# Moving the memory values ahead of the attention, reordering a router, moving a branch, and keeping the experts' sum with features on partitions

## The chip, the cores and the metric

The kernel runs on one core of a Trainium2 chip. The metric is the time of one execution on the device, in microseconds; the time before and after is the median of several executions. A profile comes from one execution of its own. All times below are microseconds unless marked ns.

## What is computed

Two transformer blocks, one after the other, on one sequence of 256 tokens with 1024 features, in fp32. Cut to what the change touches:

```python
# first block
x = x + g1 * mixed                                  # attention (MLA and neighbourhood) @ w_out
t = modulate(rmsnorm(x, norm_ffn_g), sh2, sc2)      # rows t of 1024 features
g_sel = argmax(t @ w_rg + b_rg)                     # router: one of 4 groups
e_logits = (t @ w_re + b_re)[group g_sel]           # top 2 of the group's 4 experts
y = sum over the 2 chosen experts of weight * ((silu(t @ wg[e]) * (t @ wu[e])) @ wd[e])
x = rmsnorm(x + g2 * y, final_norm_g)
# second block
h = rms_norm(x, g_mix)
proj = h @ w_in        # convolution, stick-breaking attention, queries xq, gates
k, v = split(rms_norm(mem, g_mem) @ w_mem_kv)       # memory keys and values, 256 x 1024 each
...                    # cross attention of xq on k, v; gated sum; w_out; MLP
```

The memory keys and values depend on no result of the first block. There are 16 experts with 512 hidden features.

## The kernel before

The order of the work is written by hand: each engine runs its instructions in the order of the code, and waits where an operand isn't there. Weights come from HBM once, as pieces of about 1 MB, in the order of the list `plan`; `pump()` issues the next loads while slots of the SBUF pool are free (`take` and `give` take and return a slot of 4 KB per partition, 24 in all). SP issues them.

Most products run through a stream `S` of jobs. A piece is split into a rounded high part (line 207 on ACT, or 205 on DVE) and the rest (line 208 on DVE), and three matmuls make one product: `step` (line 233) holds the activations and moves 512 weight columns, `step_w` (line 272) holds the weights and moves 256 tokens. `S.fine` (line 252) is the same as `step`, as a generator that emits a few matmuls at a time. PSUM has eight banks: four "b" banks for short-lived results and four "acc" banks for accumulation; a new tile of a kind waits until the oldest user of its bank is done.

The stages, in order: adaLN and memory keys, with the first half of the memory values; `w_in` products of the first block (the last job is nv); attention by heads, with `latents()` as side work; `w_out` (J_wo[0], J_wo[1]); router; 16 experts in pairs; the second block.

- The second half of the memory values is the job J_mv[1]. It is loaded after w_out and emitted in portions between the steps of the router by `fill(n)` (lines 1075, 1084, 1128, 1192), and goes to HBM by line 1193.
- `router_const()` (line 856) multiplies the shift sh2 with the router's weights (16 matmuls of 20 columns) and adds the result to `br` (line 861). It is called last in `latents()`.
- Router: `xa_T(c)` transposes x (features to partitions) and scales it; `logits` (line 1049) accumulates 20 columns; line 1107 scales them to `lg`; lines 1117 to 1126 rank groups and experts on DVE; lines 1131 to 1133 count with matmuls into the bank `bl`; line 1136 makes the place of each token in its expert's list, and `slots_of(n)` (line 1143) the one-hot map `D[n]` of four experts; `tot` (line 1148) reads `bl` last. An expert has 64 places.
- `xn` is x divided by its root mean square, `xh` and `xlo` its high part and rest (GpSimd, line 1104); their columns are reordered. `gather(n)` (line 1181) multiplies them with `D[n]` into `xg[n]`, tokens of four experts, features on partitions; two "b" banks at a time.
- `bcast_rows(i, t)` (line 981) spreads a row of the modulation over all partitions by matmuls of one row; the one of g2 into `gm` is in expert 1.
- Experts: `moe_up` (line 1269), gate (lines 1283, 1284), `moe_hT`, `moe_down` (line 1303), `moe_out` (lines 1317 to 1320: weighted outputs RA, split to RB), `moe_comb(p)` (line 1328) adds a pair's outputs to the sum with the map `DT`. The sum `yb[tt][dh]` has tokens on partitions and fills the four "acc" banks. `add_x` (line 1063) adds the residual x to it by a matmul with the identity.
- `beyond()` (line 1402) is a branch on a flag that says whether an expert has more tokens than places; its body isn't entered for these inputs. It stands after expert 14 (`e == NE - 2`). All engines pass line 1404 together.
- Tail: the sum is copied to x (lines 1540, 1541), `fgm` is the product of two norm gains (line 1543), GpSimd multiplies x by `fgb` (line 1548), x is transposed (line 531), `hilo` (lines 546 on ACT, 547 on DVE) makes its halves `uh`, `ul`, and `S.step()` begins the `w_in` products of the second block, into "acc" banks. Then the sums of squares, the root and its broadcast `rb`.

Of the kernel before, what the change touches and what calls it, by code (L numbers as in the profile page):

```python
# [9 lines left out]
F32 = mybir.dt.float32  # L10
# [79 lines left out]
def body(tc, d, out, dbg=None, stop=None):  # L90
# [87 lines left out]
    class Stream:  # L178
# [63 lines left out]
        def fine(self, job):  # L242

            while self.pos < job.end:
                job, key, a, k, kg, first, last, done = self.g[self.pos]
                s = self.prepared.pop(self.pos)
                if first:
                    job.accs = job.acc()
                for m, (hi, lo) in enumerate(job.lhs):
                    for kk in range(kg):  # L250
                        for j, (x, w) in enumerate(((hi, 0), (lo, 0), (hi, 1))):
                            T.matmul(job.accs[m], x(k + kk), s[:, w, kk, :], start=first and kk == 0 and j == 0,  # L252
                                     stop=last and kk == kg - 1 and j == 2)
                    if last:
                        job.evac(m, job.accs[m])
                    if m == len(job.lhs) - 1:
                        give(s)
                        self.pos += 1
                    yield

# [157 lines left out]
    plan_mod(1, range(4, 8))  # L418
    P_uq = [plan_w(("uq", c), d["w_uq"], 384, 384 * c, 384) for c in range(2)]
# [6 lines left out]
    P_memv.append(plan_w(("mv", 1), d["w_mem_kv_2"], 1024, 1536, 512))  # L426
# [166 lines left out]
    J_mv = [Job(P_memv[c], 512, mlhs, ev_memv(c), acc=(lambda: [bank(), bank()]) if c else None) for c in range(2)]  # L593
# [161 lines left out]
    for j in (J_kvl, J_ql, J_nq, J_nk, J_nv):  # L755
        S.add(j)
# [84 lines left out]
    give(*hT["x"], *hT["c"])  # L841
    dump("nqT", nqT)
# [24 lines left out]
    def latents():  # L867
# [37 lines left out]
        router_const()  # L905
# [95 lines left out]
    for j in J_wo + J_mv[1:]:  # L1001
        S.add(j)
# [32 lines left out]
    def xa_T(c):  # L1035
        for k0, bk in transposed_pairs(lambda tt, k: x[:, tt, 512 * c + k:512 * c + 512:4], 4):
# [72 lines left out]
    keep(1)  # L1109
# [18 lines left out]
    fill(1)  # L1128
# [17 lines left out]
    slots_of(0)  # L1146
    tot = smal([128, 16], "tot")
# [755 lines left out]
```

## Time and profile before

| what | value |
|---|---|
| median of three runs | 1071.27 (1068.00 to 1072.09) |
| the profiled execution's own time | 1069.21 |
| span of the profile | 1067.4 |
| granted TensorE clock over the span | 0.992 |
| PE busy | 1037.5 (97%) |
| DVE, ACT, POOL busy | 593.8 (56%), 437.4 (41%), 92.4 (9%) |
| HBM read | 249.73 MB |

The span runs from the first to the last instruction of the profiled execution; the 1.8 us around it are in that execution's own time. Matmuls of one group overlap their neighbours by a little in the rows, since their ends are modelled: the pace of a stretch is read from the starts of its groups. L12 is line 12 of the kernel before.

### The profile page before, as it was taken

How to read it: one execution, taken by the hardware profiler on the slowest of the kernel's cores; microseconds unless marked ns; L12 is line 12 of the kernel's file. 1: busy time of each engine (PE TensorE's matmuls, PEld its weight loads, DVE VectorE, ACT ScalarE, POOL GpSimd, SP SyncE). 2: the span in 40 equal slices, each digit the busy share in tenths (PEclk: the TensorE clock that was granted, in tenths of full speed). 3: DMA queues.
4: the chain of work that ended last, by engine and by line, in shares of the span. 5: the costliest groups of instructions: out<-in, count | busy, mean ns of one | idle time of the engine just before them, and what ended most of it. 6: DMA issues, size and time to landing. Idle time of an engine off the chain costs nothing.

```text
span 1067.4 us, 14961 instructions
## 1 busy us (share of the span) xinstructions
PE 1037.5 (97%) x6035; PEld 777.6 (73%) x6035; DVE 593.8 (56%) x928; ACT 437.4 (41%) x744; POOL 92.4 (9%) x100
## 2 busy tenths in 40 slices
PE   6999999999999999998999999999999999999998
PEld 5587866657744343433699789998888889999996
DVE  5565237775624342523666556766456677666544
ACT  5664115674423131312534684444443144443332
POOL 0000303000201010100104452000000000000000
PEclk9999999999999999999999999999999999999999
DMA  9999741625789999999924324537566555455511
GB/s 333 402 354 346 222 150 54 251 105 240 273 344 419 418 419 420 419 419 412 383 70 160 129 78 151 175 119 260 174 204 229 197 197 197 160 196 201 193 41 40
DMA packets 82410, 254.95 MB, mean 239 GB/s; under 512 B 4760, under 2 KB 8344, under 8 KB 67616
## 3 DMA queue, kind: packets, MB, share of 16 engines
q1 hardware_dynamic: 80848, 249.22, 62.7%
q0 software_dynamic: 1488, 4.72, 1.4%
q8 instruction: 49, 0.80, 0.3%
q14 instruction: 25, 0.20, 0.1%
HBM read 249.73 MB, written 4.19 MB: 238 GB/s over the span
## 4 chain that ended last, share of the span: by engine, by line
PE 73%; DMA 19%; DVE 4%; ACT 2%; SPq 1%; issue 1%; DVEq 0%; ACTq 0%
PE acc L233 35%; PE acc L272 14%; DMA raw<-in_w_up 9%; PE b L272 8%; DMA raw<-in_w_down 6%; PE b L1269 3%; PE b L531 2%; DMA raw<-in_w_mod 2%; PE b L640 2%; DMA raw<-in_w_in 1%; PE acc L964 1%; PE b L252 1%; SPq L141 1%; DVE split L208 1%; DVE sm L940 1%; PE b L1610 1%
## 5 line engine op out<-in xcount | busy, mean ns | idle before, releaser
L208 DVE TENSOR_TENSOR split<-raw,split 128x1024 fp32r<-128x1024 f32 (+2 forms) x226 | 267.8, 1212 | 92.7 <-ACT split L207 90.5
L207 ACT ACTIVATE split<-raw 128x1024 fp32r<-128x1024 f32 (+2 forms) x170 | 168.7, 1034 | 63.0 <-DMA raw<-in_w_uq 15.7
L272 PE MATMUL acc<-uh,split 128*128 128x256 f32 x640 | 123.2, 288 | 1.4 <-ACT uh L546 1.4
L1269 PE MATMUL b<-raw,xg 128*64 128x512 f32 x512 | 116.1, 602 | 3.8 <-DVEq L1404 3.8
L272 PEld LDWEIGHTS acc<-uh,split 128*128 128x128 f32 x640 | 102.5, 193 | 2.7 <-ACT uh L546 1.8
L233 PE MATMUL acc<-split,uh 128*128 128x512 f32 x320 | 101.3, 392 | 0.0
L272 PE MATMUL b<-fh,split 128*128 128x256 f32 x512 | 93.8, 283 | 0.3 <-DVE split L208 0.3
L272 PE MATMUL acc<-ul,split 128*128 128x256 f32 x320 | 91.3, 285 | 0.1
L233 PE MATMUL acc<-split,hidT 128*128 128x512 f32 x384 | 88.4, 389 | 0.0
L1269 PEld LDWEIGHTS b<-raw,xg 128*64 128x64 f32 x512 | 35.8, 138 | 71.7 <-issue 69.9
L233 PEld LDWEIGHTS acc<-split,hidT 128*128 128x128 f32 x384 | 71.6, 188 | 14.6
L272 PEld LDWEIGHTS b<-fh,split 128*128 128x128 f32 x512 | 80.4, 192 | 0.8 <-DVE split L208 0.5
L272 PE MATMUL b<-fl,split 128*128 128x256 f32 x256 | 72.4, 283 | 0.0
L233 PEld LDWEIGHTS acc<-split,uh 128*128 128x128 f32 x320 | 60.1, 188 | 12.8
L272 PEld LDWEIGHTS acc<-ul,split 128*128 128x128 f32 x320 | 61.9, 193 | 0.7 <-DVE ul L547 0.6
L233 PE MATMUL acc<-split,ul 128*128 128x512 f32 x160 | 62.3, 390 | 0.0
L1303 PE MATMUL b<-raw,RA 128*64 128x512 f32 x256 | 58.5, 596 | 1.2 <-DMA raw<-in_w_down 1.2
L1317 DVE SCALAR_TENSOR_TENSOR RA<-b,wc,gm 64x512 f32<-64x512 f32 x32 | 24.0, 750 | 60.4 <-PE b L1303 59.9
L1318 ACT ACTIVATE RB<-RA 64x512 fp32r<-64x512 f32 x32 | 20.1, 628 | 77.6 <-DVE RA L1317 77.5
L272 PEld LDWEIGHTS b<-fl,split 128*128 128x128 f32 x256 | 49.1, 192 | 0.3
L1830 ACT ACTIVATE hid<-b 128x512 f32<-128x512 f32 x16 | 9.5, 595 | 91.3 <-PE b L272 91.3
L1303 PEld LDWEIGHTS b<-raw,RA 128*64 128x64 f32 x256 | 17.8, 137 | 37.6 <-issue 32.2
(414 smaller groups left out, 1738.7 us busy)
## 6 DMA issues: line engine op xcount, KB each, us to landing
raw<-in_w_up SPq DMA_DIRECT2D x48, 1024.0 KB, 13.2
raw<-in_w_down SPq DMA_DIRECT2D x48, 1024.0 KB, 16.2
raw<-in_w_in SPq DMA_DIRECT2D x46, 1024.0 KB, 7.5
raw<-in_w_gate SPq DMA_DIRECT2D x32, 1024.0 KB, 19.8
raw<-in_w_mod SPq DMA_DIRECT2D x24, 1024.0 KB, 8.2
raw<-in_w_out SPq DMA_DIRECT2D x8, 1024.0 KB, 6.1
raw<-in_w_mem_kv SPq DMA_DIRECT2D x7, 1024.0 KB, 11.1
raw<-in_w_conv_out SPq DMA_DIRECT2D x4, 1024.0 KB, 5.1
```

The costliest lines, as they stand in the source:

```text
L141: nc.sync.dma_start(t, src)
L207: A.activation(s[:, 0], src, AF.Copy)
L208: V.tensor_tensor(s[:, 1], src, s[:, 0].bitcast(F32), op=OP.subtract)
L233: T.matmul(job.accs[m], x(k + kk), s[:, w, kk, :], start=job.start and first and kk == 0 and j == 0, stop=job.stop and last and kk == kg - ...
L252: T.matmul(job.accs[m], x(k + kk), s[:, w, kk, :], start=first and kk == 0 and j == 0, stop=last and kk == kg - 1 and j == 2)
L272: T.matmul(bk[:, o:o + 256], s[:, w, kk, 128 * b:128 * b + 128], x(k + kk), start=first and b % per == 0 and r == 0 and kk == 0 and j == 0 ...
L531: T.transpose(bk[0:m, i * 128:i * 128 + p], s, ident)
L640: T.matmul(modacc[Tn][32 * g:32 * g + 32, :], cond[:, k, :], w[:, g // 2, 512 * (g % 2):512 * (g % 2) + 512] if Tn == 2 else w[:, g, :], s ...
L1269: T.matmul(b[64 * j:64 * j + 64, :], lt, raw((nm, e, k // 4))[:, k % 4, :], start=(k == 0), stop=(k == 7), skip_group_check=True)
L1303: T.matmul(b[64 * j:64 * j + 64, :], t[:, k, :], raw(("d", e, k // 2))[:, k % 2, 512 * dh:512 * dh + 512], start=(k == 0), stop=(k == 3), ...
L1317: V.scalar_tensor_tensor(RA[r, dh, :], b[r, :], wc[r, dh, e % 2:e % 2 + 1], gm[r, dh], op0=OP.mult, op1=OP.mult)
L1318: A.activation(RB[r, 0, dh, :], RA[r, dh, :], AF.Copy)
```

## The change

The job J_mv[1] moves into the stream behind nv, ahead of the attention, and its loads move with it; `fill` and `fine` go. `router_const()` moves to the start of the router, `add_x(0)` to `add_x(3)` and the broadcast of g2 into it. `xn` goes: `x_hi` (ACT) and `x_lo` (DVE) make the halves from x, without reordering; the gather takes every fourth column instead. The first gather uses four "b" banks at once and takes the parts that need the last rest at the end. The experts' sum becomes `yT`, features on partitions: `moe_comb` holds 128 columns of RB and moves 256 columns of DT. The first `sq` job of the second block accumulates in "b" banks. The branch and its hint move from expert 14 to expert 13. In the tail, `hilo` reads the sum directly, and `y_back` transposes it to tokens on partitions afterwards, for the sum of squares and the product with `fgb`. The branch's body (not entered) is adapted to the new layout and left out here.

```diff
...
+    P_memv.append(plan_w(("mv", 1), d["w_mem_kv_2"], 1024, 1536, 512))
     P_uq = [plan_w(("uq", c), d["w_uq"], 384, 384 * c, 384) for c in range(2)]
...
-    P_memv.append(plan_w(("mv", 1), d["w_mem_kv_2"], 1024, 1536, 512))
...
-    for j in (J_kvl, J_ql, J_nq, J_nk, J_nv):
+    for j in (J_kvl, J_ql, J_nq, J_nk, J_nv, J_mv[1]):
...
+    mvt[1] = take([128, 2, 512], F32, "mvt")
+    S.run(J_mv[1])
+    G.dma_start(mvd[:, :, 512:1024], mvt[1])
+    give(memTh, memTl, mvt[1])
...
         give(st["kvl"], st["kvT"])
-        router_const()
...
     def xa_T(c):
-        for k0, bk in transposed_pairs(lambda tt, k: x[:, tt, 512 * c + k:512 * c + 512:4], 4):
+        bks = [bank() for _ in range(2)]
+        for tt in range(2):
+            for k in range(4):
+                o = 256 * (k % 2) + 128 * tt
+                T.transpose(bks[k // 2][:, o:o + 128], x[:, tt, 512 * c + k:512 * c + 512:4], ident)
...
-    yb = [[None, None], [None, None]]
-    xres = x
-    def add_x(tt, dh):
-        T.matmul(yb[tt][dh], ident, xres[:, tt, 512 * dh:512 * dh + 512], start=False, stop=False, skip_group_check=True)
+    yT = [None] * 4
+    def y_of(k):
+        return yT[k // 2][:, 256 * (k % 2):256 * (k % 2) + 256]
+    def add_x(k, first=False):
+        if first and k % 2 == 0:
+            yT[k // 2] = bank("acc")
+        for tt in range(2):
+            T.matmul(y_of(k)[:, tt * 128:(tt + 1) * 128], x[:, tt, k * 128:(k + 1) * 128], ident,
+                     start=first and k % 2 == 0 and tt == 0, stop=False, skip_group_check=True)
     la[0] = 4
     S.run(J_wo[1])
     la[0] = 2
-    mvt[1] = take([128, 2, 512], F32, "mvt")
-    mvg = S.fine(J_mv[1])
-    def fill(n):
-        for _ in range(n):
-            next(mvg, None)
-    fill(3)
+    router_const()
...
-    fill(2)
-    logits(1, 0)
-    logits(1, 1)
+    add_x(0, True)
+    add_x(1, True)
+    logits(1, 0, 1)
     give(xaT)
     keep(4)
-    xn = take([128, 2, 1024], F32, "xn2")
+    gm = take([128, 4, 512], F32, "gm")
     xh = take([128, 2, 1024], F32R, "xh")
     xlo = take([128, 2, 1024], F32R, "xlo")
     keep(1)
-    def fo(t):
-        return t.rearrange("p (h j q) -> p h j q", h=2, j=4)
-    def fi(t):
-        return t.rearrange("p (h q j) -> p h j q", h=2, j=4)
-    V.tensor_scalar(fo(xn[:, 0, :]), fi(x[:, 0, :]), r2[:, 0:1], None, op0=OP.mult)
-    for tt in range(2):
-        A.activation(fo(xh[:, tt]), fi(x[:, tt, :]), AF.Identity, scale=r2[:, tt:tt + 1])
-    A.activation(fo(xn[:, 1, :]), fi(x[:, 1, :]), AF.Identity, scale=r2[:, 1:2])
-    for tt in range(2):
-        G.tensor_tensor(xlo[:, tt], xn[:, tt], xh[:, tt].bitcast(F32), op=OP.subtract)
+    def x_hi(hi):
+        for tt in range(2):
+            A.activation(hi[:, tt], x[:, tt, :], AF.Identity, scale=r2[:, tt:tt + 1])
+    def x_lo(hi, lo):
+        for tt in range(2):
+            V.scalar_tensor_tensor(lo[:, tt], x[:, tt, :], r2[:, tt:tt + 1], hi[:, tt].bitcast(F32), op0=OP.mult, op1=OP.subtract)
+    x_hi(xh)
     lg = smal([128, 2, 20], "lg")
     for tt in range(2):
         V.scalar_tensor_tensor(lg[:, tt], lgb[:, 20 * tt:20 * tt + 20], r2[:, tt:tt + 1], br, op0=OP.mult, op1=OP.add)
     dump("lg", lg)
-    keep(1)
+    add_x(2, True)
+    add_x(3, True)
+    bcast_rows(1, gm)
...
-    fill(1)
     bl = bank()
...
     slots_of(0)
+    x_lo(xh, xlo)
     tot = smal([128, 16], "tot")
     V.tensor_reduce(tot, bl[:, 32:64].rearrange("p (t e) -> p e t", t=2), AX.X, OP.add)
...
     def halves(n):
         hi, lo = take([128, 2, 1024], F32R, "xh"), take([128, 2, 1024], F32R, "xlo")
-        for tt in range(2):
-            A.activation(hi[:, tt], xn[:, tt], AF.Copy)
-            G.tensor_tensor(lo[:, tt], xn[:, tt], hi[:, tt].bitcast(F32), op=OP.subtract)
+        x_hi(hi)
+        x_lo(hi, lo)
...
+        def part(q, bks, i):
+            h, tt = (xh, xh, xlo, xlo)[i], i % 2
+            for k in range(4):
+                T.matmul(bks[k // 2][:, 256 * (k % 2):256 * (k % 2) + 256],
+                         h[:, tt, 512 * q + k:512 * q + 512:4], Dn[tt],
+                         start=(i == 0 and k % 2 == 0), stop=(i == 3), skip_group_check=True)
...
+        if n == 0:
+            bq = [[bank(), bank()] for _ in range(2)]
+            for i in range(3):
+                for q in range(2):
+                    part(q, bq[q], i)
+            for q in range(2):
+                part(q, bq[q], 3)
+                evac(q, bq[q])
+            return
+        for q in range(2):
+            bks = [bank(), bank()]
+            for i in range(4):
+                part(q, bks, i)
+            evac(q, bks)
             yield
-    fill(8)
-    G.dma_start(mvd[:, :, 512:1024], mvt[1])
-    give(memTh, memTl, mvt[1])
...
     def moe_comb(p):
         for dh in range(2):
-            for tt in range(2):
-                if p == 0:
-                    yb[tt][dh] = bank("acc")
-                for w in range(2):
-                    T.matmul(yb[tt][dh], DT[:, (2 * dh + tt) * 128:(2 * dh + tt + 1) * 128], RB[:, w, dh, :],
-                             start=(p == 0 and w == 0), stop=(p == 7 and w == 1), skip_group_check=True)
+            for w in range(2):
+                for i in range(4):
+                    k = 4 * dh + i
+                    if p == 0 and w == 0 and k in (4, 6):
+                        yT[k // 2] = bank("acc")
+                    T.matmul(y_of(k), RB[:, w, dh, 128 * i:128 * i + 128], DT[:, 256 * dh:256 * dh + 256],
+                             start=(p == 0 and w == 0 and k in (4, 6)), stop=(p == 7 and w == 1), skip_group_check=True)
...
+            J2[nm, c] = Job(P_in2[nm, c], 512, evac=ev_sqk(nm == "sk", c), rhs=urhs,
+                            acc=(lambda: [bank(), bank()]) if (nm, c) == ("sq", 0) else None)
...
+        if e == NE - 3:
+            tc.mark_branch_hint_location("over", "LikelyTaken", engines=[mybir.EngineType.PE])
...
-                gm = take([128, 4, 512], F32, "gm")
-                bcast_rows(1, gm)
...
-        if e == NE - 2:
+        if e == NE - 3:
             beyond()
...
-    add_x(0, 0)
+    add_x(4)
+    add_x(5)
     moe_down(NE - 2)
-    add_x(1, 0)
     moe_down(NE - 1)
-    add_x(0, 1)
-    add_x(1, 1)
+    add_x(6)
+    add_x(7)
     raw_done("x")
     S.hold = None
     S.ahead(1)
+    fgm = smal([128, 8], "fgm")
+    V.tensor_tensor(fgm, col("final_norm_g"), col("g_mix_2"), op=OP.mult)
     moe_comb(NE // 2 - 1)
     give(gm, RA, RB)
-    x = take([128, 2, 1024], F32, "x1")
     lim[:] = [4, 2]
     ss3 = smal([128, 4], "ss3")
-    for tt in range(2):
-        A.activation(x[:, 0, 512 * tt:512 * tt + 512], yb[0][tt], AF.Copy)
-        V.tensor_copy(x[:, 1, 512 * tt:512 * tt + 512], yb[1][tt])
...
-    xf = take([128, 2, 1024], F32, "x1f")
-    for tt in range(2):
-        G.tensor_tensor(xf[:, tt], x[:, tt], fgb, op=OP.mult)
     uh = s2["uh"] = take([128, 8, 256], F32R, "uh")
     ul = s2["ul"] = take([128, 8, 256], F32R, "ul")
-    for k0, bk in transposed_pairs(lambda tt, k: x[:, tt, k * 128:(k + 1) * 128], 8):
-        for kk in range(2):
-            hilo(uh[:, k0 + kk], ul[:, k0 + kk], bk[:, kk], fgm[:, k0 + kk:k0 + kk + 1])
-        if k0:
-            S.step()
-        if 0 < k0 < 6:
-            tt = k0 // 2 - 1
-            sumsq(ss3[:, tt:tt + 1], x[:, tt, :])
-    give(x)
-    x = xf
+    yt = take([128, 8, 256], F32, "yt")
+    x = take([128, 2, 1024], F32, "x1f")
+    def y_halves(dh):
+        for k in range(4 * dh, 4 * dh + 4):
+            hilo(uh[:, k], ul[:, k], y_of(k), fgm[:, k:k + 1])
+            if k in (1, 3):
+                S.step()
+        A.activation(yt[:, 4 * dh:4 * dh + 2].rearrange("p a t -> p (a t)"), yT[2 * dh], AF.Copy)
+        V.tensor_copy(yt[:, 4 * dh + 2:4 * dh + 4].rearrange("p a t -> p (a t)"), yT[2 * dh + 1])
+    def y_back(dh):
+        s = slice(512 * dh, 512 * dh + 512)
+        for tt in range(2):
+            bk = trans_bank([yt[:, 4 * dh + i, tt * 128:(tt + 1) * 128] for i in range(4)])
+            sumsq(ssh[:, dh, tt:tt + 1], bk)
+            V.tensor_tensor(x[:, tt, s], bk, fgb[:, s], op=OP.mult)
+    y_halves(0)
+    y_halves(1)
+    y_back(0)
+    S.step()
+    y_back(1)
+    give(yt)
+    V.tensor_tensor(ss3[:, 0:2], ssh[:, 0], ssh[:, 1], op=OP.add)
...
```

## Rows read from the trace of the kernel before

**Rows 1.** Windows: length; busy PE, PEld, DVE, ACT, POOL; granted clock; DMA share; GB/s.
```profile
280.00:300.00 20.00, 17.36 (x90) 14.41 (x91) 10.44 (x34) 11.97 (x16) 5.46 (x3) 0.83 0.67 231
...
480.00:500.00 20.00, 15.78 (x68) 4.81 (x64) 6.97 (x11) 4.91 (x7) 0.00 (x0) 0.91 1.01 416
```

**Rows 2.** Chain of waits that ended last, two of its links (columns: start; us; link).
```profile
107.02 5.94 PE acc L272 x48
...
134.78 5.68 PE acc L233 x24
```

**Rows 3.** Timeline in the attention (columns: start; us; engine; line; operation; idle before).
```profile
205.74 1.86 PE L859 MATMUL acc<-wr,sh 128*128 128x20 f32 x16
...
207.96 0.17 DVE L861 TENSOR_TENSOR br<-br,acc 128x20 f32<-128x20 f32 x1
...
208.69 0.43 DVE L938 TENSOR_TENSOR b<-b,raw 128x256 f32<-128x256 f32 x1 [0.57 <-PE b L926]
...
210.78 1.13 PE L929 MATMUL b<-kT,qT 96*128 96x512 f32 x2 [1.09 <-DVE b L938]
```

**Rows 4.** Timeline of the router, w_out's end to the first expert.
```profile
274.77 0.39 PE L252 MATMUL b<-split,memTh 128*128 128x512 f32 x1
...
284.22 2.40 POOL L1104 TENSOR_TENSOR xlo<-xn,xh 128x1024 fp32r<-128x1024 f32 x1 [4.79 <-ACT xh L1101]
...
284.88 1.92 DVE L1117 TENSOR_TENSOR cmp<-lg 128x160 f32<-128x160 f32 x1
...
286.72 0.31 DVE L1118 TENSOR_TENSOR cmp<-lg 128x160 f32<-128x160 f32 x1
...
288.56 0.61 PE L1131 MATMUL b<-selm,cst 128*128 128x32 f32 x2 [2.64 <-DVE selm L1126]
...
289.83 0.77 PE L252 MATMUL b<-split,memTh 128*128 128x512 f32 x1
...
290.28 0.90 DVE L1143 TENSOR_TENSOR D<-cst,posm 128x512 fp32r<-128x512 f32 x1
...
295.10 1.23 PE L1181 MATMUL b<-D,xh 128*128 128x256 f32 x8
...
298.98 10.52 PE L1269 MATMUL b<-raw,xg 128*64 128x512 f32 x48
```

**Rows 5.** Granted clock of one microsecond, PE alone (columns: stretch; length; PE; clock; DMA; GB/s).
```profile
254.00:255.00 1.00, 1.00 (x4) 0.71 1.05 442
```

**Rows 6.** Timeline: the two broadcasts of rows.
```profile
251.78 2.13 PE L981 MATMUL acc<-grow,ones 1*128 1x512 f32 x4
...
309.43 1.13 PE L981 MATMUL b<-grow,ones 1*128 1x512 f32 x4
```

**Rows 7.** Timeline around the branch, PE and DVE.
```profile
470.57 0.68 DVE L1284 TENSOR_TENSOR gm<-b,gm 64x512 f32<-64x512 f32 x1 [0.96 <-ACT gm L1283]
...
471.80 3.65 PE L1269 MATMUL b<-raw,xg 128*64 128x512 f32 x16
...
484.84 1.41 DVE L1320 TENSOR_TENSOR RB<-RA,RB 64x512 fp32r<-64x512 f32 x2
...
486.99 5.09 PE L1269 MATMUL b<-raw,xg 128*64 128x512 f32 x16 [3.76 <-DVEq L1404]
```

**Rows 8.** Timeline behind the branch: a wait for weights.
```profile
494.45 1.94 PE L1303 MATMUL b<-raw,RA 128*64 128x512 f32 x8 [0.46 <-DMA raw<-in_w_down]
```

**Rows 9.** Timeline of the tail; the last row is tile fgm's view (ns min/median/max).
```profile
507.65 1.13 PE L1063 MATMUL acc<-raw,cst 128*128 128x512 f32 x2
...
514.71 1.90 PE L1328 MATMUL acc<-RB,DT 128*128 128x512 f32 x7 [0.21 <-DVE RB L1320]
...
515.59 1.22 DVE L208 TENSOR_TENSOR split<-raw,split 128x1024 fp32r<-128x1024 f32 x1 [0.21 <-ACT split L207]
...
519.84 0.39 PE L272 MATMUL acc<-uh,split 128*128 128x256 f32 x1 [1.39 <-ACT uh L546]
...
L547 DVE SCALAR_TENSOR_TENSOR ul<-b,fgm,uh x8: 477/484/484, 519.8 to 530.6; 128x256 fp32r<-128x256 f32 x8
```

More of the change, by code (lines that the diff above doesn't have):

```diff
@@ L240, in step @@
             self.pos += 1
[L242 to L259, printed above, removed]
         def step_w(self, job, s, k, kg, first, last):
@@ L592, in body @@
     J_mk = [Job(P_memk[c], 512, mlhs, ev_memk(c)) for c in range(2)]
-    J_mv = [Job(P_memv[c], 512, mlhs, ev_memv(c), acc=(lambda: [bank(), bank()]) if c else None) for c in range(2)]
+    J_mv = [Job(P_memv[c], 512, mlhs, ev_memv(c)) for c in range(2)]
     for j in J_mk + J_mv[:1]:
@@ L1000, in body @@
     J_wo = [Job(P_wo[c], 512, wol, ev_wo(c)) for c in range(2)]
-    for j in J_wo + J_mv[1:]:
+    for j in J_wo:
         S.add(j)
@@ L1035, in xa_T @@
     def xa_T(c):
-        for k0, bk in transposed_pairs(lambda tt, k: x[:, tt, 512 * c + k:512 * c + 512:4], 4):
+        bks = [bank() for _ in range(2)]
[3 more added lines that the diff above has]
+                T.transpose(bks[k // 2][:, o:o + 128], x[:, tt, 512 * c + k:512 * c + 512:4], ident)
+        for k0 in (0, 2):
+            bk = bks[k0 // 2].rearrange("p (k t) -> p k t", k=2)
             for kk in range(2):
@@ L1176, in gather, with evac @@
         Dn = [D[n][:, tt].rearrange("p e c -> p (e c)") for tt in range(2)]
-        for q in range(2):
-            bks = [bank() for _ in range(2)]
-            for i, (h, tt) in enumerate(((xh, 0), (xh, 1), (xlo, 0), (xlo, 1))):
-                for k in range(4):
-                    T.matmul(bks[k // 2][:, 256 * (k % 2):256 * (k % 2) + 256],
-                             h[:, tt, (4 * q + k) * 128:(4 * q + k + 1) * 128], Dn[tt],
-                             start=(i == 0 and k % 2 == 0), stop=(i == 3), skip_group_check=True)
+        def part(q, bks, i):
[4 more added lines that the diff above has]
+                         start=(i == 0 and k % 2 == 0), stop=(i == 3), skip_group_check=True)
+        def evac(q, bks):
             for k in range(4 * q, 4 * q + 4):
@@ L1404, in beyond @@
         with tc.If(flag > 0, label="over"):
-            hb = take([128, 2, 512], F32, "hb")
+            hbb = take([128, 2048], F32, "hb")
+            hb = hbb[:, 0:1024].rearrange("p (t n) -> p t n", t=2)
+            hbT = hbb[:, 1024:2048].rearrange("p (k t) -> p k t", k=4)
             xb = take([128, 2, 1024], F32, "xb")
@@ L1415, in beyond @@
             give(xb)
-            hbT = take([128, 4, 256], F32, "hbT")
             for e in range(NE):
@@ L1438, in beyond @@
                     A.activation(hbT[:, k0:k0 + 2], bk, AF.Copy)
-                for tt in range(2):
-                    for dh in range(2):
+                for dh in range(2):
+                    for i in range(4):
                         for k in range(4):
-                            T.matmul(yb[tt][dh], hbT[:, k, tt * 128:(tt + 1) * 128], wd[dh][:, k, :], start=False,
+                            T.matmul(y_of(4 * dh + i), wd[dh][:, k, 128 * i:128 * i + 128], hbT[:, k, :], start=False,
                                      stop=False, skip_group_check=True)
                 give(*wd)
-            give(hb, hbT, h2T)
+            give(hbb, h2T)
         A.preload_act_table_set("silu_and_others")
     for e in range(NE):
-        if e == NE - 2:
-            tc.mark_branch_hint_location("over", "LikelyTaken", engines=[mybir.EngineType.PE])
         if e == NE - 3:
@@ L1506, in body @@
             pump()
-        if e == NE - 2:
+        if e == NE - 3:
             beyond()
@@ L1515, in body @@
             junk[0] = cp.tile([128, 1024], BF, name="junkB", tag="junk")
-            give(xn)
             lim[:] = [99, 0]
@@ L1531, in body @@
     S.ahead(1)
+    fgm = smal([128, 8], "fgm")
+    V.tensor_tensor(fgm, col("final_norm_g"), col("g_mix_2"), op=OP.mult)
     moe_comb(NE // 2 - 1)
     give(gm, RA, RB)
-    x = take([128, 2, 1024], F32, "x1")
     lim[:] = [4, 2]
     ss3 = smal([128, 4], "ss3")
-    for tt in range(2):
-        A.activation(x[:, 0, 512 * tt:512 * tt + 512], yb[0][tt], AF.Copy)
-        V.tensor_copy(x[:, 1, 512 * tt:512 * tt + 512], yb[1][tt])
-    fgm = smal([128, 8], "fgm")
-    V.tensor_tensor(fgm, col("final_norm_g"), col("g_mix_2"), op=OP.mult)
+    ssh = smal([128, 2, 2], "ssh")
     fgb = raw("fgb")
-    xf = take([128, 2, 1024], F32, "x1f")
-    for tt in range(2):
-        G.tensor_tensor(xf[:, tt], x[:, tt], fgb, op=OP.mult)
     uh = s2["uh"] = take([128, 8, 256], F32R, "uh")
     ul = s2["ul"] = take([128, 8, 256], F32R, "ul")
-    for k0, bk in transposed_pairs(lambda tt, k: x[:, tt, k * 128:(k + 1) * 128], 8):
-        for kk in range(2):
-            hilo(uh[:, k0 + kk], ul[:, k0 + kk], bk[:, kk], fgm[:, k0 + kk:k0 + kk + 1])
-        if k0:
-            S.step()
-        if 0 < k0 < 6:
-            tt = k0 // 2 - 1
-            sumsq(ss3[:, tt:tt + 1], x[:, tt, :])
-    give(x)
-    x = xf
+    yt = take([128, 8, 256], F32, "yt")
[20 more added lines that the diff above has]
+    V.tensor_tensor(ss3[:, 0:2], ssh[:, 0], ssh[:, 1], op=OP.add)
     for tt in range(2):
```

1 line of the change is left out of this document (removed).

## The prediction, made before the changed kernel was built or run

> **What bounds the kernel now.** I read the page's busy times first: PE is busy 97% of the span (table above), so in most stretches a PE instruction taken away or added counts in full, and the change can only gain where PE is idle, at half clock, or does work that goes away. Then the windows. At 280 to 300 us (router) PE is busy 17.36 of 20 at a granted clock of 0.83; at 480 to 500 us 15.78 of 20, with the DMA share at 1.01 and 416 GB/s [rows 1]. These two are the weak stretches that the diff touches. Then the timeline of each, to see which wait ends last, and the chain of waits for the pace of plain matmul stretches: 24 matmuls of 512 columns in 5.68 us, 0.237 each; 48 of 256 columns in 5.94 us, 0.124 each [rows 2].
>
> Times below are those of the profiled execution: 1069.21 us with a span of 1067.4. The median of the three runs, 1071.27, is 2.06 higher.
>
> **A. The memory values go ahead of the attention: +11.4.** The second half of the values is 48 matmuls of 512 columns. Before, they fill the router's waits; after, they stand in the weight stream behind the nv job, where PE is already full. 48 × 0.237 = 11.4. A faster pace, such as 0.227 in the router's own copies (18 from 274.77 on, at the full clock) [rows 4], would give 10.9. The write to HBM and the four slots given back early are on queues that nobody waits for here.
>
> **B. router_const leaves the attention: −0.7.** It holds PE from 205.74 to 207.53, 1.79 us. But DVE is the engine that the heads wait for: it is idle 0.57 before line 938 because the scores of line 926 came late, and spends 0.17 on line 861. The next matmul waits 1.09 for DVE [rows 3]. 0.57 + 0.17 = 0.74. Bounds: 0, if DVE is late elsewhere, and −1.86, if PE's share counts in full.
>
> **C. The shorter router: −5.8.** Before, from the first fill matmul at 274.77 to the first expert matmul at 298.98 it is 24.2 us [rows 4], 11.4 or more of it the fill matmuls. After, without them, I lay the chain out from t = 0, the end of w_out:
> - router_const 1.8 (beside it the residual, x and the sum of squares), eight transposes of 128 columns, some 0.9 (at most 8 × 0.124) → 2.7; their evacuation, two pieces of 256 columns on each of two engines at 0.48 as line 547 [rows 9], with add_x(0), (1) on PE beside it, 0.9 → 3.6; logits 1.8 (16 small matmuls, as router_const's [rows 3]) → 5.4; the scaled logits → 5.9.
> - DVE's ranks: seven operations. Line 1117 takes 1.92, its twin line 1118 takes 0.31 [rows 4], while GpSimd's subtraction of line 1104 ran until 286.6; that subtraction is gone, so I count 0.31 and 2.0 for the group, → 8.0. Had line 1117 its 1.92 for another reason, 1.6 more. PE has add_x(2), (3) and bcast_rows meanwhile (some 2.0), so both are hidden; uncovered they would cost those 2.0.
> - Counts and map: from 288.56 to 290.28 the six count matmuls and posm, 1.7 at the lower clock, then 0.90 for D [rows 4]. At the full clock I take 1.2 and, with the way to the next engine, 1.1 → 10.3.
> - Then x_lo on DVE: two operations over 1024 elements. Line 547, the same form, takes 0.484 for 256; line 208, a two-operand one, 1.22 for 1024 [rows 9]. I take 1.25 each (bounds 1.2 and 1.9) → 12.8; `tot` behind it 0.2 → 13.1. The gather wants four "b" banks at once; one of them is bl, which only `tot` releases, and `tot` stands behind x_lo. So PE does six or so matmuls and waits for 13.1. Before, `tot` followed D at once, and the fill matmuls lay between.
> - 26 of the 32 gather matmuls at 0.121 (32 from 295.10 to 298.98 [rows 4]): 3.1 → 16.2, and 0.2 for an evacuation → 16.4.
> - Half clock: PE is idle while it waits for the ranks and for `tot`. Before, after 2.64 idle, twelve matmuls from 289.83 to 295.10 took 0.44 each, not 0.227: 2.6 lost [rows 4]; after the branch sixteen took 5.09, not 3.65: 1.4 lost [rows 7]. I take 2.0, → 18.4.
>
> 24.2 − 18.4 = 5.8. Without the bank wait (1.9) and the half clock (2.0) it would be −9.7; with line 1117 slow and x_lo at 1.9 each, near −2.9.
>
> **D. bcast_rows(1) leaves expert 1: −1.06**, from 309.43 to 310.49 on PE [rows 6]. Only the DVE work behind it moves too.
>
> **E. The experts' sum with features on partitions: +0.6.** A pair's sum was 8 matmuls of 512 columns, 8 × 0.237 = 1.90; it is 16 of 256, 16 × 0.124 = 1.98 [rows 2]. Seven pairs: 7 × 0.08 = 0.6. The gathers' strided columns of xh and halves' step from POOL to DVE I cost at nothing: weight loads and DVE have room (DVE 6.97 of 20 in the expert window [rows 1]); if the strides slowed every load by 0.03, 128 × 0.03 = 3.8 would come on top.
>
> **F. The branch behind expert 13: −4.8.** PE sits idle 3.76 at 486.99, released by DVE's own arrival at line 1404; DVE gets there only when line 1320 ends at 486.25, the outputs of pair 6. Then sixteen matmuls take 5.09 where 3.65 is normal [rows 7]. Behind expert 13 DVE's last piece is line 1284, done at 471.25, and PE goes on at 471.80 after the sum. PE went on 0.74 after DVE's last work, so it would go on at 472.0: 0.2 to 0.4 idle and no half clock. −(3.76 + 1.44 − 0.4) = −4.8. The stall moved, what is late next is the weights: PE waits 0.46 for a w_down piece at 494.45 [rows 8], because PE ran ahead while 1.05 MB comes every 2.5 us at 416 GB/s. Freed memory (the two mem slots, two raw pieces of mv, xn) lets four to five pieces load earlier, which I take as enough: that wait goes too, **−0.5**; not enough, it takes 2 back.
>
> **H. The tail: −0.4.** One add_x of 1.05 between the last two moe_downs [rows 9] goes ahead (−1.05 or, with the shorter ones, −0.9). The first matmul of block two came at 519.84, 3.3 after the sum's end near 516.5: copies, transposes and hilo in a row, with fgm on DVE between them. After, hilo reads the sum itself, so some 516.5: −3.3. But this is given back: the eight hilo pairs (DVE's half 0.48 each [rows 9]) still feed PE, ACT and DVE take turns on each bank, splits of 1.22 on DVE stand between them, the sum of squares comes only after y has been transposed back (16 transposes beside the stream instead of 8 ahead of it, two banks only), and x's multiplication is on DVE now, so that the row broadcasts that end this stretch come when they came before. Bounds −3 and +2.
>
> **Sum.** 11.4 − 0.7 − 5.8 − 1.06 + 0.6 − 4.8 − 0.5 − 0.4 = −1.3. On the profiled run: 1067.9; on the median: 1070.0. I say 1069.
>
> **The rivals.**
> 1. Faster, 1061. The clock stays up in the router (−2.0), bl's bank is not among the first needed (−1.9), router_const counts in full (−1.1), and the tail keeps 2 more: −1.3 − 7.0 = −8.3. For it: PE's longest wait before, 2.64 [rows 4], is cut up. Against: the clock also fell where PE did not wait, behind four matmuls of one row at 251.78: 0.71 from 254 to 255, with PE busy throughout [rows 5, 6].
> 2. Slower, 1074. The same observation turned round: the router's small work (20-column logits, transposes, one-row bcast) takes PE to the lower clock already before the ranks. Then logits +1.8, add_x and bcast end 1.1 after the ranks, counts +0.65, the gather's rest +1.1: 4.7 more, +3.4: 1072.6 on the profiled run, 1074.7 on the median. It decides from the point where the clock has fallen by the logits. Against: sixteen such matmuls ran in 1.86 in the attention without it [rows 3].
> 3. The branch does not gain. The stall is that of the branch itself, and goes with it wherever it stands: −1.3 + 4.8 = +3.5, 1073. Against: DVE's arrival ended PE's wait, and DVE arrived late for a reason that the rows show [rows 7].
>
> The Trainium skill, "Runtime: NRT & Kernel Launch", section "Instruction fetch mechanics", says that a taken branch whose target has not been prefetched forces a fetch before execution goes on. By that rule the stall would follow the branch, as in rival 3; the trace does not bear it out, since PE's wait ended 0.74 after DVE's last work.
>
> 4. It does not do what it says: the matmuls of A are no filler lost but needed cover, so all of C's waits open up (each bound above against me, C at −2.9, H at +2): 1073 to 1075 again.
>
> **Chances.** Forecast 0.45 (1066 to 1071), rival 1 0.27, rival 2 0.13, rival 3 0.1, rival 4 0.05. The range of 8 in 10 takes in the fast case and most of the slow ones: 1061 to 1075. About 0.5%, 5.4 us, is what a measurement of this kernel can tell from no change. Faster by more than that needs most of rival 1: 0.27. Slower by more needs 1076.7, two bad terms together: 0.13. Same: 0.60.
>
> **What would show it.** Right: 48 more L233 matmuls ahead of the attention at 0.23; PE's wait before the ninth gather matmul or so, released by DVE's `tot`; the branch's PE wait under 0.5 behind expert 13's gate; the first block-two matmul 0.2 to 0.5 behind the sum. Wrong: granted clock below 0.8 through the whole router (rival 2); a PE wait of 3 or more at the branch (rival 3); a DMA wait in experts 14 and 15 above 1 us; a second matmul wait in the tail of over 2 us.

## The result, and the profile after

The changed kernel takes 1077.75 us (median; 1077.40 to 1078.06), the one before 1071.49 in the same runs: a ratio of 1.0069 [1.0053, 1.0085]. The ratios here are worked out over all executions, with a 95% interval, and differ a little from those of the medians (here 1.0058). I had forecast 1069, down by 0.2%, in a range up to 1075. It is slower by 0.6 to 0.7%, outside the range. The profiled execution took 1077.40, with a span of 1075.6 against 1067.4: 8.2 more.

I cut both timelines at work that exists in both, at the start of the first matmul of each piece of work, on PE:

| stretch | before | after | difference |
|---|---|---|---|
| start to the first memory product | 9.80 | 9.38 | −0.42 |
| to the first attention scores (48 more matmuls of the memory values) | 151.59 | 161.96 | +10.37 |
| to the first transposes of P (the products of uq and ukv) | 15.17 | 16.28 | +1.11 |
| heads, to the first w_out matmul | 66.25 | 65.73 | −0.52 |
| w_out, to its last matmul | 31.74 | 31.72 | −0.02 |
| from there (router) to the first expert matmul | 24.43 | 18.97 | −5.46 |
| to the first sum of a pair | 37.08 | 35.88 | −1.20 |
| experts and tail, to block two's first matmul | 183.78 | 184.68 | +0.90 |
| first w_in jobs of block two | 26.42 | 29.62 | +3.20 |
| the rest, to the end of PE's last matmul | 517.18 | 517.42 | +0.24 |

Most rows are as the sum had them. The experts are not: they should have lost 4.8 at the branch, 0.5 of waiting for weights, 1.05 of add_x and, up to this edge, 3.3 in the tail, and gained 0.6 in the sums of pairs. They did lose about that, and something took it back. It stands in the timeline of PE in the experts of the kernel after (start, us, engine, line, operation), at each of the three gathers there. This is the first of them:

```profile
341.91 2.04 PE L1169 MATMUL b<-D,xh 128*128 128x256 f32 x8
343.78 2.05 PE L1169 MATMUL b<-D,xlo 128*128 128x256 f32 x8
345.67 0.66 PE L1296 MATMUL b<-cst,gm 128*128 128x128 f32 x4
346.08 2.11 PE L1169 MATMUL b<-D,xh 128*128 128x256 f32 x8
348.04 2.02 PE L1169 MATMUL b<-D,xlo 128*128 128x256 f32 x8
349.90 0.26 PE L1244 MATMUL b<-cw,RA 128*128 128x6 bf16 x4
```

From 341.91 to 349.90 it is 7.99. The same stretch of the kernel before:

```profile
338.03 1.08 PE L1181 MATMUL b<-D,xh 128*128 128x256 f32 x8
338.94 1.07 PE L1181 MATMUL b<-D,xlo 128*128 128x256 f32 x8
...
342.57 0.25 PE L1242 MATMUL b<-cw,RA 128*128 128x6 bf16 x4
```

4.54. The three later gathers take 7.99, 7.97 and 8.00 after, 4.54, 4.66 and 4.60 before: +10.2 in all. PE counts as busy all the while, and no wait shows, since the cost lies in the instruction itself. One has to look at the weight loads (LDWEIGHTS, on PEld: they bring the operand that a matmul holds). By line (ns min/median/max), first the gather before, then after:

```profile
L1181 PEld LDWEIGHTS b<-D,xh x64: 187/188/330, 294.7 to 445.9; 128*128 128x128 f32 x64
```

```profile
L1169 PEld LDWEIGHTS b<-D,xh x64: 309/330/334, 295.2 to 458.8; 128*128 128x128 f32 x64
```

Same shape, same type: 188 ns where the 128 columns lie side by side, 330 where every fourth one is loaded (16 bytes apart). With the longer loads the pace goes from 0.115 to 0.235 a matmul. (The rows of neighbouring loads overlap, so that a load's duration is not its price; the pace is.)

The router, which answers to [rows 4], came out as forecast (18.75 from router_const's first matmul, where my t = 0 lay, against 18.4), but not by my working:

```profile
285.30 1.86 PE L844 MATMUL acc<-wr,sh 128*128 128x20 f32 x16
...
293.32 0.38 PE L1119 MATMUL b<-selm,cst 128*128 128x32 f32 x2 [0.50 <-DVE selm L1115]
...
295.25 1.75 PE L1169 MATMUL b<-D,xh 128*128 128x256 f32 x6 [1.10 <-DVE D L1131]
297.74 2.70 PE L1169 MATMUL b<-D,xh 128*128 128x256 f32 x10 [0.74 <-DVE tot L1137]
300.24 3.87 PE L1169 MATMUL b<-D,xlo 128*128 128x256 f32 x16
304.04 17.39 PE L1271 MATMUL b<-raw,xg 128*64 128x512 f32 x80
```

Counts at 8.0 from the stage's start, map at 10.0, then six matmuls and the wait for `tot`: as laid out. The 26 that are left take 6.30, 0.24 each. The granted clock (length; PE busy; clock; DMA; GB/s) is at 0.50 in part of the stretch, so that this looks like the 2.0 that I had counted for the lower clock:

```profile
293.00:297.00 4.00, 2.58 (x12) 0.78 0.43 177
297.00:301.00 4.00, 3.26 (x15) 0.50 0.00 0
301.00:305.00 4.00, 4.00 (x20) 0.87 0.72 262
```

But the pace stays at 0.24 when the clock has come back (0.98 to 1.00 from 302 to 304). Here the two costs lie over each other.

The branch and the tail, which answer to [rows 7] and [rows 9]:

```profile
484.96 3.19 PE L1271 MATMUL b<-raw,xg 128*64 128x512 f32 x13 [0.41 <-PEq L1408]
488.96 1.07 PE L1271 MATMUL b<-raw,xg 128*64 128x512 f32 x3 [0.81 <-issue]
...
520.98 2.52 PE L1331 MATMUL acc<-DT,RB 128*128 128x256 f32 x16 [0.42 <-ACT RB L1320]
524.60 0.38 PE L253 MATMUL b<-uh,split 128*128 128x256 f32 x1 [1.10 <-ACT uh L527]
```

The wait at the branch is 0.41, at the full clock, and the wait for w_down at 494.45 [rows 8] has gone. There is a new one of 0.81 with no releaser in sight. From the last sum to block two's first matmul it is 3.62 instead of 5.96.

### The profile page after: what moved, and what is told of

Its sections match the earlier page's. It is cut to its first block, busy times and chain, and to the rows that moved or that the text cites. A ratio compares the mean times of both kernels' runs of the same rounds, so it can differ in the third digit from the quotient of the medians.

```text
span 1075.6 us, 15125 instructions
## 1 busy us (share of the span) xinstructions
PE 1048.3 (97%) x6123; PEld 796.0 (74%) x6123; DVE 601.7 (56%) x940; ACT 434.2 (40%) x747; POOL 68.8 (6%) x90
## 4 chain that ended last, share of the span: by engine, by line
PE 51%; DVE 2%; ACT 1%; issue 1%; DVEq 0%; ACTq 0%
PE acc L233 26%; PE acc L253 9%; PE b L253 8%; PE b L1271 1%; PE b L1305 1%; DVE split L208 1%; PE b L1621 1%; PE b L1643 1%; PE b L512 1%; PE b L1699 1%; PE b L1723 1%; ACT junkB L505 0%; PE b L1654 0%; PE acc L1331 0%; ACT split L207 0%
## 5 line engine op out<-in xcount | busy, mean ns | idle before, releaser
L253 PE MATMUL acc<-uh,split 128*128 128x256 f32 x576 | 109.6, 286 | 0.0
L253 PEld LDWEIGHTS acc<-uh,split 128*128 128x128 f32 x576 | 91.4, 192 | 0.8 <-issue 0.3
L253 PE MATMUL acc<-ul,split 128*128 128x256 f32 x288 | 81.5, 283 | 0.0
L253 PEld LDWEIGHTS acc<-ul,split 128*128 128x128 f32 x288 | 55.2, 192 | 0.1
L233 PE MATMUL acc<-split,memTh 128*128 128x512 f32 x128 | 43.1, 407 | 1.5 <-DVE split L208 1.4
## 6 DMA issues: line engine op xcount, KB each, us to landing
raw<-in_w_down SPq DMA_DIRECT2D x48, 1024.0 KB, 10.8
raw<-in_w_gate SPq DMA_DIRECT2D x32, 1024.0 KB, 12.4
```

The lines of the kernel that those rows point to most:

```text
L233: T.matmul(job.accs[m], x(k + kk), s[:, w, kk, :], start=job.start and first and kk == 0 and j == 0, stop=job.stop and last and kk == kg - ...
L253: T.matmul(bk[:, o:o + 256], s[:, w, kk, 128 * b:128 * b + 128], x(k + kk), start=first and b % per == 0 and r == 0 and kk == 0 and j == 0 ...
```

## The experiments

The theory: the strided weight loads cost what the forecast lacks, some 10 us, and the other terms stand. The first rival: the gathers are slow for another reason (the halves on DVE, the banks). The second: the weights from HBM bound the experts, and a faster PE only waits.

**Columns side by side again.**

```diff
     def x_hi(hi):
-            A.activation(hi[:, tt], x[:, tt, :], AF.Identity, scale=r2[:, tt:tt + 1])
+            A.activation(fo(hi[:, tt]), fi(x[:, tt, :]), AF.Identity, scale=r2[:, tt:tt + 1])
...
-                         h[:, tt, 512 * q + k:512 * q + 512:4], Dn[tt],
+                         h[:, tt, (4 * q + k) * 128:(4 * q + k + 1) * 128], Dn[tt],
```

> The changed kernel, but the halves of x are written in the reordered form of before, so that the gather loads 128 columns that lie side by side instead of every fourth one (the subtraction on DVE is four instructions of 512 elements instead of two of 1024). Theory (the strided weight loads cost the time: 0.330 us a load, 0.233 a matmul, where before it was 0.188 and 0.115): the three later gathers go back from 8.0 to 4.6 us each, -10.2; the first gather is at the lower clock and gives 0 to 3 more. About 1067, at most 1068, at least 1064: faster than before. Rival 1 (the gather is slow for another reason, the halves made on DVE or the banks): 8.0 stays, 1077 to 1078. Rival 2 (the weights from HBM bound the experts, so that faster gathers only wait for weights): the gain stays under 5, 1073 to 1075, with waits on w_up, w_gate or w_down in the experts.

Measured: 1075.27, ratio 1.0055 [1.0030, 1.0080]. The time lies just above the second rival's, but no wait for weights of more than 0.4 does it; the loads did what the theory says: 188 ns, and the gather from 346.25 to 350.89 takes 4.64. The time is not told apart from the changed kernel's 1.0069, and misses the theory's 1064 to 1068: the price had moved. Now ACT and DVE read x at every fourth element, and new waits appear. Rows of the kernel: the subtraction by tile (512 elements each), ACT's high part, and two lines of PE's waits (us in total, times, longest):

```profile
L1096 DVE SCALAR_TENSOR_TENSOR xlo<-raw,r_r,xh x16: 1123/1157/1202, 296.4 to 447.6; 128x512 fp32r<-128x512 f32 x16
L1091 ACT ACTIVATE xh<-raw,r_r x8: 2115/2184/2238, 291.2 to 444.2; 128x1024 fp32r<-128x1024 f32 x8
...
PE acc L1339 <- ACT DT L1266: 4.9, 3, 1.7
...
PE b L1177 <- DVE tot L1145: 2.6, 1, 2.6
```

DVE takes 1.157 for 512 elements, where the kernel after takes 1.280 for 1024; ACT 2.18 instead of 1.14. The longer halves hold ACT, so the pair's map DT comes late three times, and `tot` stands behind four subtractions of 1.16. The experts still gain 6.5 (178.21 in the table's row, not 184.68), the router loses 1.9.

**The stride, put into the kernel before.** With the step in the gather, x's halves are no longer reordered.

```diff
     def fo(t):
-        return t.rearrange("p (h j q) -> p h j q", h=2, j=4)
+        return t
...
-                             h[:, tt, (4 * q + k) * 128:(4 * q + k + 1) * 128], Dn[tt],
+                             h[:, tt, 512 * q + k:512 * q + 512:4], Dn[tt],
```

> The kernel before, with one thing changed: x's halves are kept in x's own order and the gather loads every fourth column. Theory (strided loads): 3 x 3.4 = 10.2 more in the later gathers, up to 3.7 more in the first, 1 back from waits for weights that go: 1081 to 1085. Rival (stride costs nothing by itself): 1071 to 1072.

Measured: 1081.48 against 1067.90, ratio 1.0115 [1.0087, 1.0144], +12.3 by the ratio. Loads 329 ns:

```profile
L1181 PEld LDWEIGHTS b<-D,xh x64: 308/329/337, 296.4 to 459.9; 128*128 128x128 f32 x64
```

The first gather, here at the full clock, takes 7.5 instead of 3.9, the first of the later ones 7.88 instead of 4.54, and the experts 191.70 instead of 183.78. Of the 12.3, 1.2 is a side effect: the wait for the ranks in the router is 3.80 instead of 2.64. So the stride costs more than the whole change loses, with the halves made on the same engines and the banks used as before. That excludes the first rival.

**Every second column.** The halves are written so that two of the four interleaved columns lie together (one instruction for each pair, `g`), and the gather's step is 2.

```diff
...
-                         h[:, tt, 512 * q + k:512 * q + 512:4], Dn[tt],
+                         h[:, tt, 512 * q + 256 * (k // 2) + k % 2:512 * q + 256 * (k // 2) + 256:2], Dn[tt],
```

> The changed kernel, with the halves of x written so that the gather loads every second column (8 bytes apart) instead of every fourth (16 bytes). It is to tell what the load's price hangs on. If any stride halves the rate of a load: 0.330 us a load again, 1077 to 1079. If the price grows with the distance: between 0.188 and 0.330, about 0.24, the three gathers at 5.5 to 6.5 us, 1071 to 1074. If only 16 bytes cost: 0.188, as with columns side by side, 1067 to 1069.

Measured: 1069.06, ratio 1.0009 [0.9993, 1.0024]: no difference from before. The load takes 197 ns, close to 188, and the gather goes at 0.120 a matmul:

```profile
L1179 PEld LDWEIGHTS b<-D,xh x64: 193/197/333, 294.7 to 449.6; 128*128 128x128 f32 x64
```

So the third of the readings: 8 bytes apart is nearly free, 16 bytes make the load three quarters longer. The span falls from 1075.6 to 1065.6, 10.0, the experts' row from 184.68 to 175.21, 9.5. (By the ratios it is 6.4; 1.5 of the span is w_out, which varies between executions, as told at the end.) One flaw is left: the subtraction is eight instructions of 0.48 now, and PE waits 1.6 for `tot`.

With that, the change without its stride makes no difference that can be measured. The sum said −1.3, just beyond the interval's end of −0.7. The next runs ask whether its terms are right one by one.

**The branch alone, in the kernel before.** Its hint goes along, and two buffers of its body, which is not entered, become one.

```diff
...
-        if e == NE - 2:
+        if e == NE - 3:
             beyond()
```

> The kernel before, with the branch and its hint behind expert 13 and the branch body's two buffers in one (the body isn't entered). Theory (PE waited for DVE's late arrival and then ran at the lower clock): -3.8 - 1.4 + 0.8 = -4.4, 1067. Rival 1 (the stall belongs to the branch): 0, 1071. Rival 2 (the weights bound the last experts, since here no memory was freed for earlier loads): waits on w_down and w_up take back most, -0.5 to -2, 1069.5 to 1071.

Measured: 1069.72 against 1067.90, ratio 1.0010 [0.9995, 1.0025]. The second rival: the wait has only moved.

```profile
471.19 3.65 PE L1269 MATMUL b<-raw,xg 128*64 128x512 f32 x16 [0.40 <-PEq L1404]
...
483.11 3.65 PE L1269 MATMUL b<-raw,xg 128*64 128x512 f32 x16 [0.49 <-DMA raw<-in_w_up]
490.58 5.43 PE L1303 MATMUL b<-raw,RA 128*64 128x512 f32 x16 [3.82 <-DMA raw<-in_w_down]
```

0.40 at the branch instead of 3.76, and 3.82 for w_down two steps later, with the lower clock behind it. So the stall at the branch is gone, and the gain of the move depends on the weights being there.

**The branch back behind expert 14, in the kernel of every second column.**

```diff
...
-        if e == NE - 3:
+        if e == NE - 2:
             beyond()
```

> The kernel of e4 (the change with a gather of every second column), with the branch and its hint back behind expert 14. It asks what the branch's new place is worth where memory was freed, since in the kernel before the same move only turned the stall into waits for weights (w_down, 4.6 us). Theory (the place is worth 4.4 if the weights are there): 4 to 5 above e4, so about 1.005 of before, with a PE wait of 3.5 to 4 at the branch and 1.4 of lower clock behind it. Rival (the experts end when the weights have come, wherever the branch stands): within 1 of e4, 0.999 to 1.002 of before.

Measured: 1072.27, 1.0031 [1.0015, 1.0046] of before, against 1.0009 [0.9993, 1.0024]: +0.2%, between the two readings, and the intervals overlap. The traces decide: the experts' row grows from 175.21 to 178.66, 3.45. The wait is back:

```profile
492.72 5.35 PE L1281 MATMUL b<-raw,xg 128*64 128x512 f32 x16 [3.76 <-DVEq L1418]
```

Here, with memory freed early, the place is worth 3.45: not my 4.8, since behind expert 13 PE waits 0.41 and, 13 matmuls later, 1.08 without a releaser.

**The memory values alone, in the kernel before.** The plan's entry goes ahead of uq, too, the job accumulates in "acc" banks, and all `fill` calls go.

```diff
-    for j in (J_kvl, J_ql, J_nq, J_nk, J_nv):
+    for j in (J_kvl, J_ql, J_nq, J_nk, J_nv, J_mv[1]):
...
     give(*hT["x"], *hT["c"])
+    mvt[1] = take([128, 2, 512], F32, "mvt")
+    S.run(J_mv[1])
+    G.dma_start(mvd[:, :, 512:1024], mvt[1])
+    give(memTh, memTl, mvt[1])
```

> The kernel before, with the memory values alone moved ahead of the attention (loads, products, the write and the memory given back), and no fill matmuls in the router; nothing else changed. Price by the change's trace: 48 x 0.2325 = 11.2 more ahead of the attention and 1 for the splits of uq. The router without fills: my chain gives 17 to 18 instead of 24.2, limited by GpSimd's subtraction (line 1104). Waits for weights in the experts (1.2) go, since four slots are free earlier. Theory: 11.2 + 1.0 - 6.5 - 1.2 = +4.5, 1.004 of before. Rival (the fills were all cover: the router is bound by ACT, GpSimd and DVE, and gets no shorter than 21): +8, 1.007 of before.

Measured: 1077.68 against 1069.76, ratio 1.0077 [1.0049, 1.0105]: the rival. Ahead of the attention it costs 11.6 + 1.2 (0.5 of it before any of the moved work, where executions of the same code differ as much); the router shrinks from 24.43 to 19.55 only, neither to the theory's 17 to 18 nor as little as the rival's 21, and waits open in it:

```profile
290.84 3.43 PE L1053 MATMUL acc<-wr,xaT 128*128 128x20 f32 x16
299.00 0.60 PE L1125 MATMUL b<-selm,cst 128*128 128x32 f32 x2 [4.73 <-DVE selm L1121]
...
302.05 2.05 PE L1175 MATMUL b<-D,xh 128*128 128x256 f32 x8 [1.59 <-DVE tot L1142]
```

(Of the 7.8 in span, 1.2 lies behind PE's last matmul, for no reason that I found.) Of 11.2 of fill, 6.3 was cover. Without it, the logits run at the lower clock (3.43 instead of 1.86). What the change's router gains beyond this comes from its own edits: it does 4.7 more work (router_const, four add_x, the broadcast) in 0.6 less.

**`tot` ahead of the subtraction, in the kernel of every second column.**

```diff
     slots_of(0)
-    x_lo(xh, xlo)
     tot = smal([128, 16], "tot")
     V.tensor_reduce(tot, bl[:, 32:64].rearrange("p (t e) -> p e t", t=2), AX.X, OP.add)
+    x_lo(xh, xlo)
```

> The kernel of e4 with the sum tot put ahead of x_lo on DVE, so that the bank of the counts is released before the subtraction. Theory (PE waits 1.6 for tot, and the rest of the gather then runs at the lower clock): the sixteen matmuls on the high part run at once, and only the last ones wait for x_lo: 2 to 3 below e4, 0.998 to 1.000 of before. Rival (x_lo ends the gather anyway): the wait on tot turns into one on xlo of about the same length, within 0.7 of e4.

Measured: 1067.49, ratio 0.9984 [0.9968, 0.9999] of before. The router goes from 19.63 to 17.14: −2.5, as the theory says.

**The memory values back in the router, in that kernel.** The five lines that the run of the memory values alone had added go, the loads go back behind w_out, and `fine` comes back.

```diff
     router_const()
+    fill(1)
...
+    fill(1)
     logits(1, 0, 1)
...
+    fill(6)
     slots_of(0)
...
```

> The kernel of e6 with the second half of the memory values back in the router as fill (6 matmuls behind router_const, 6 ahead of the logits, 36 behind the counts) and its loads behind w_out, as before. 12 us go from ahead of the attention; 11.2 come back in the router less the idle time and the lower clock that they cover there (2 to 5). Theory (the freed memory pays for the branch's place): waits on w_down and w_up of 3 to 5 come back in the last experts, so 0 to -2 against e6. Rival (the loads are early enough): -3 to -5 against e6, the fastest of all, 0.994 to 0.997 of before.

Measured: 1069.16, ratio 0.9997 [0.9984, 1.0010]. 11.0 + 1.1 go ahead of the attention, 10.8 come back in the router (27.92 instead of 17.14), and 4.8 in the experts, where w_down is late:

```profile
PE b L1343 <- DMA raw<-in_w_down: 2.6, 1, 2.6
```

It is 1.4 slower by the ratios, whose intervals overlap, and 2.2 by the spans, beyond the theory's end and away from the rival's. In these traces the early memory values pay by the 4.8 in the experts, as the memory that they free lets weights load earlier; without that they would cost.

**The broadcast back in expert 1, in the kernel with `tot` first.**

```diff
     add_x(3, True)
-    bcast_rows(1, gm)
...
             if e == 1:
+                bcast_rows(1, gm)
```

> The kernel of e6 with the broadcast of g2 (four matmuls of one row) back in expert 1, as before. In e6 the counts and the gather's sixteen matmuls on the high part run at the lower clock (0.50 from 293 to 297), right behind this broadcast and two short waits. Theory (the one-row matmuls bring the clock down): without them the counts and the gather run at the full clock, -0.6 - 1.9, and 1.06 comes back in expert 1: -1.4 against e6, 0.997 of before. Rival (the short waits and small matmuls of the router bring it down without the broadcast too): the lower clock stays, the wait for the ranks grows from 0.5 to 1.6, and expert 1 gets 1.06 longer: +1 against e6, 0.999 to 1.000 of before.

Measured: 1066.64 against 1068.17, ratio 0.9980 [0.9969, 0.9992], the lowest ratio of all, 0.2% below before and clear of it by its interval; not told apart from the kernel with the broadcast in the router (0.9984). The clock, first there, then here:

```profile
289.00:293.00 4.00, 3.49 (x26) 0.97 1.01 420
293.00:297.00 4.00, 2.90 (x14) 0.50 0.70 293
297.00:301.00 4.00, 4.00 (x25) 0.67 0.22 33
```

```profile
289.00:293.00 4.00, 3.64 (x33) 1.00 1.01 419
293.00:297.00 4.00, 1.70 (x10) 0.89 1.02 429
297.00:301.00 4.00, 4.00 (x26) 0.69 0.44 125
```

Both readings are half right. Without the broadcast the counts run at the full clock, and the router is 1.0 shorter; the clock falls all the same, later, behind the waits of 1.56 and 1.10; and expert 1 takes 1.2 back.

## Why the prediction was wrong, point by point

**E is the step that failed.** I wrote: "The gathers' strided columns of xh and halves' step from POOL to DVE I cost at nothing: weight loads and DVE have room", with an upper end of 0.03 a load, 3.8. It is 0.12 a matmul, 10.2 in the 96 matmuls of the three later gathers. What I put at nothing sets the gather's pace: it is 0.115 with loads of 188 ns, 0.120 with 197, 0.235 with 330. Two mistakes are in it. First, room: PEld is busy 4.81 of 20 us in the window I cited, but that window has no gather in it, and what counts is one load beside one matmul. Second, a sign of the price was in the trace of before, and I did not read it. There, `xa_T` transposes with every fourth column as weights, among the transposes of the same tile:

```profile
L531 PEld LDWEIGHTS b<-cst,raw x36: 138/142/212, 53.7 to 279.6; 128*128 128x128 f32 x36
```

142 is the median, 212 the longest. In the kernel after, those transposes have a line of their own:

```profile
L1024 PEld LDWEIGHTS b<-cst,raw x16: 196/212/259, 274.1 to 287.8; 128*128 128x128 f32 x16
```

I had looked at the pace of these transposes, which hardly shows it: 0.120 with every fourth column, 0.109 with columns side by side. 0.07 more a load, over 128 loads, would have been 9.

The Trainium skill has the rule, in "Advanced Engine Details and Errata", section "SBUF Cachelines": lines are 16 bytes, and accesses that each go to another line are slower; at least two hits on a line are needed. The traces agree: one element in 16 bytes 330 ns, two 197, four 188. It was the rule against this change, and I had not weighed it.

The other terms, by the table and the runs:

- **A**, +11.4: 48 matmuls at 0.2325, 11.2. Right; but the products behind them waited 1.0 more for the splits of uq, which I had not seen, so 12.2. (The table's two rows show 11.5, because the stretch ahead of the `w_in` products was 0.7 shorter in this execution. The stretch from there to the scores is 99.1 in every kernel without the early memory values and 110.2 in every one with them.)
- **B**, −0.7: −0.5. Right.
- **C**, −5.8: −5.5, right by luck. The ranks were as laid out (0.33 for the operation that took 1.92 before, the subtraction 1.28). But the gather went on behind `tot` at 12.4 after the stage's start, not 13.1, and the last 26 matmuls took 6.3, not the 5.3 that I had for them, the evacuation and the clock. The stride was hidden in that: with columns side by side the same 26 took 5.8, at the lower clock.
- **D**, −1.06: −1.2. Right.
- **F**, −4.8 and −0.5: in the trace of the change PE's stretch from the sum ahead of the branch (469.75 before, 482.47 after) to the next add_x goes from 33.32 to 28.91, −4.4, with the wait of 0.46 for w_down in it, so that the place itself is nearer to 3.5 to 4 than to 4.8; two more such waits ahead of it (0.23 and 0.55) went too. The mechanism (DVE's late arrival) is shown by the two branch runs; a stall of 3.76 that goes with the branch, rival 3, is excluded: the wait at the branch is 0.4 behind expert 13 and 3.76 behind expert 14 in either kernel. A smaller cost of the branch is not: see the open point at the end. That freed memory is what lets the gain stay was argued in half a sentence. The runs bear it out: 3.82 of wait for w_down where the branch moved alone, none in the change, 2.57 where the memory values went back into the router.
- **H**, −0.4: −1.2 from add_x, −2.3 up to block two's first matmul, +3.2 after it: −0.35. Right, give-back included; but the −0.4 was a guess, since I gave the give-back no number.

Without E's gathers the table's rows add to −2.0, of which 1.1 lies ahead of any work that the change touches; my sum was −1.3 with its 0.6 for the sums of pairs, which measured 0. (The sum gave 1070.0 on the median; the 1069 lies between that and the profiled execution's 1067.9.) Rival 2's clock fell only behind the counts (1.00 up to 295, 0.61 from 295 to 296), and rival 1's did not stay up; neither decided. Rival 4's waits opened where the memory values alone were moved (+8), not in the change, which has work of its own in the router. No rival held the stride, so the range ended at 1075.

## What to carry to other kernels

A change of layout is priced at every reader: here one reordered copy in the router had been paying for 128 weight loads, and moving the stride to ACT and DVE in the reordering of each half gave no time back that could be told (1.0055 against 1.0069). Look for the nearest row with the same step, at the duration of the instruction itself, since the pace of another stretch can hide it; a step of two fp32 was nearly free for the loads (197 ns against 188) where a step of four was not (330). And a stall that was taken away while HBM was saturated (418 GB/s) came back as a wait for weights, unless memory was freed early enough to load ahead.

## What was not expected of the hardware

- The w_out stretch takes 31.7 in some executions and 30.15 in others, whatever the kernel (31.74 before, 31.72 after, 30.18 with every second column, 30.14 with the branch alone moved): behind the four one-row matmuls the clock falls to 0.50 for some 3 us in some and stays at 1.00 in others. The kernel with `tot` first and the last one have the same code up to there and took 30.16 and 31.72. That is 1.6 between executions, and in a comparison of two traces it has to be taken out by hand.
- At the lower clock the strided load costs the gather little: in the first gather of the change the pace is 0.25 at a clock of 0.50 and 0.24 when it rises, while with every second column and `tot` first it is 0.22 at 0.50, and with columns side by side 0.23.
- Open: the wait of 0.7 to 1.2 with no releaser, 12 or 13 matmuls behind the branch, in the six kernels of the changed layout with the branch behind expert 13. It isn't there in the kernel before with the same place of the branch, nor with the branch behind expert 14. The trace gives a hint. Queue q8, of kind instruction, moves 16 KB for every 250 or so of PE's instructions; around the branch there is one more (in the change from 486.58 to 487.53, with the next at 492.66), and in all six PE goes on 1.3 to 1.6 us after it has landed (here at 488.96). So PE may be waiting for its instructions, a cost of the branch; no run was made to show it.
